# The copy of q's and k's transposes queued two half chunks behind them, and the transposes five half chunks behind the rotation

## The chip, the cores and the metric

The kernel runs on one core of one Trainium2 chip. The metric is the device time of one execution in microseconds, a median of three runs.

## The reference

One trunk layer on 256 rows of 2048 numbers, all in float32. The part in which the change lies is the projection and the attention:

```
xn = rms_norm(h, norm1_g[l])
proj = jnp.einsum('bsd,dn->bsn', xn, w_in[l].astype(xn.dtype))
q, k, v, ga, gg = jnp.split(proj, ...)
q = apply_rope(rms_norm(q, q_norm_g[l]), cos, sin)
k = apply_rope(rms_norm(k, k_norm_g[l]), cos, sin)
att = diff_attention(q, k, v, lam)
att = rms_norm(att, subln_g[l]) * (1.0 - lambda_init)
u = silu(layer_norm(causal_depthwise_conv(ga * sigmoid(gg))))
h = h + concat([att, u]) @ w_out
h = h + (silu(hn @ w_gate) * (hn @ w_up)) @ w_down      # hn = rms_norm(h, norm2_g)
```

There are 4 heads; each has two pairs of q and k of 128 columns, two softmaxes that are subtracted, and 256 columns of v.

## The kernel before

Every weight matrix is streamed in chunks of two 128-row slices by 512 columns. Each chunk is rounded by ScalarE (`whi`, line 320) and the remainder is taken by VectorE (`wlo`, line 329). TensorE then multiplies a chunk in two halves: eight matmuls with `whi` (lines 359 and 360) and four with `wlo` (line 365). The casts of chunk t+2 and its remainder are queued before chunk t is multiplied; `whi` and `wlo` have three buffers each.

All the other work is written as generators. `multiply` calls `resume()` after each half of a chunk, and each running generator then puts its next instructions into the engines' queues; `lag(n)` lets n half chunks pass. So the order on each engine is fixed when the program is built, and an instruction that must wait holds everything behind it on its engine. The taps of the depthwise convolution (`y`, line 517, on VectorE) are dealt out in `run_side` between the chunks.

w_in's columns come in the order convolution, k and q of heads 0 and 1, k and q of heads 2 and 3, then v. For each block of k or q, `qk_rows` runs twice, once for each 128 rows: square sums on ScalarE (line 427), `fq` from them on GpSimd (lines 217, 218, 615), the scaled `qn` on ScalarE (line 619), the rotation on VectorE (lines 626 to 629), four transposes on TensorE (`ps_qk`, line 634), and a copy of the bank to `qT` or `kT` on ScalarE (line 635). When all of a pair of heads are placed, `attend_scores` runs per head: scores `ps_s` (line 649, two banks), their maximum on VectorE (`nmx`, line 659), exponents on ScalarE (`pr`, line 668), `r` on VectorE (line 677), `a` on GpSimd (line 679), `p` on ScalarE (line 688), the weights `wt` on VectorE (line 695), transposes `ps_wt` (line 701) and their copy to `qT` (line 706). `attend_values` then multiplies with v (`ps_o`, line 727; v is copied out of its banks at line 712), scales the result (`att`, line 738), transposes it (`ps_at`, line 746) and splits it into `mahi` on ScalarE (line 233) and `malo` on VectorE (line 234).

All these small products share four banks of PSUM (`AUX = 4`, tag `aux`). `room(n, hold)` lets a generator wait at build time until n of the four can be had, and `held` counts those that stay taken over several half chunks.

Of the kernel before, what the change touches and what calls it, by code (L numbers as in the profile page):

```python
# [63 lines left out]
RAW_BUFS = 5  # L64
AUX = 4

LAG = (3, 2, 6)
HL_BUFS = 3

KTILE_US = 1.30  # L70
# [52 lines left out]
def tile_block(  # L123
# [89 lines left out]
    def rsqrt_mean(dst, ss, n, eps):  # L213

        k = dst.shape[-1]
        t = small.tile([P, 8], F32, tag="rsq", name="rsq")
        pool.tensor_scalar(t[:, :k], ss, 1.0 / n, eps, ALU.mult, ALU.add)
        pool.tensor_tensor(dst, t[:, :k], neghalf[:, :k], ALU.pow)
# [31 lines left out]
    def lag(n):  # L250
        for _ in range(n):
            yield


    held = [0]

    def room(n, hold=0):
        while held[0] + n > AUX:
            yield
        held[0] += hold  # L260
# [6 lines left out]
    def spend(us):  # L267
        credit[0] -= us
# [156 lines left out]
    def square_sum(src, accum, **kw):  # L425
        junk = pre.tile([P, N], F32, tag="junk", name="junk", bufs=1)
        act.activation(junk[:, : src.shape[-1]], src, AF.Square, accum_out=accum, **kw)
# [162 lines left out]
    def qk_done(key, b, ps):  # L590
        for m in range(NM):
            yield
            start(qk_rows(key, b, m, ps[m]))
            yield
        if key == "q":
            while not all((k, b, m) in placed for k in "qk" for m in range(NM)):
                yield
            if b == 0:
                negative_lambda()
            for hd in (2 * b, 2 * b + 1):  # L600
                start(attend_scores(hd))
                yield from lag(4)
# [3 lines left out]
    def qk_rows(key, b, m, ps):  # L606

        G = N // DH
        spend(1.65)
        ss = small.tile([P, G], F32, tag="ssq", name="ssq")  # L610
        for j in range(G):
            square_sum(ps[:, j * DH : (j + 1) * DH], ss[:, j : j + 1], scale=rstd1[m])
        f = small.tile([P, G], F32, tag="fq", name="fq")
        rsqrt_mean(f, ss, DH, EPS)
        pool.tensor_scalar(f, f, rstd1[m], 0.0, ALU.mult, ALU.add)
        yield from lag(LAG[0])
        qn = pre.tile([P, G, DH], F32, tag="va", name="qn")
        for j in range(G):
            act.activation(qn[:, j, :], ps[:, j * DH : (j + 1) * DH], AF.Copy, scale=f[:, j : j + 1])
        yield from lag(LAG[1])  # L620
        t1 = pre.tile([P, G, DH], F32, tag="vb", name="t1")
        t2 = pre.tile([P, G, DH], F32, tag="vc", name="t2")
        tab = gcs[key, m]
        hd = DH // 2
        bc = lambda ap, n: ap.unsqueeze(1).to_broadcast([P, G, n])
        dve.tensor_tensor(t1, qn, bc(tab[:, 0, :], DH), ALU.mult)
        dve.tensor_tensor(t2[:, :, :hd], qn[:, :, hd:], bc(tab[:, 1, :hd], hd), ALU.mult)
        dve.tensor_tensor(t2[:, :, hd:], qn[:, :, :hd], bc(tab[:, 1, hd:], hd), ALU.mult)
        dve.tensor_tensor(t1, t1, t2, ALU.add)
        yield from lag(LAG[2])  # L630
        yield from room(1)
        pt = aux_ps.tile([P, G, P], F32, tag="aux", name="ps_qk")
        for j in range(G):
            pe.transpose(pt[:, j, :], t1[:, j, :], ident)
        act.copy(qkT[key][:, b * G : (b + 1) * G, m * P : (m + 1) * P], pt)
        placed.add((key, b, m))

# [609 lines left out]
```

## Time and profile before

| | |
|---|---|
| median of 3 runs | 1048.91 us (1048.85 to 1048.91) |
| the profiled execution | 1048.92 us, of which the span is 1047.1 us |
| TensorE clock granted | 1.00 |
| q, k and attention in the span | about 120 to 270 us |
| DMA, mean over the span | 221 GB/s |

A matmul's row shows a start and a length; the lengths overlap, since the next one enters while the last one drains. What counts is the distance from start to start. In brackets behind a row of the timeline stands how long the engine had nothing to do before it, and whose instruction ended that.

### The profile page before, as it was taken

The page shows a single profiled execution, that of the slowest core. Times are in us where ns is not written, and L with a number is a line of the kernel's source. Part 1 is how long each engine was busy: PE and PEld are TensorE (multiplying, and loading weights), DVE is VectorE, ACT ScalarE, POOL GpSimd, SP SyncE. Part 2 cuts the span into 40 slices and gives each one's busy share as a digit, 9 for nine tenths or more (in the row PEclk, how much of TensorE's full clock was granted, in tenths as well). Part 3 has the DMA queues.
Part 4 walks back from the last instruction along what each step waited for, and adds up shares of the span by engine and source line. Part 5 has one row for each costly group of instructions (what it writes and reads, how often), then busy time and mean ns, then how long its engine had stood idle before and what let it go on. Part 6 is the DMA issues. An engine that isn't in the chain of part 4 may idle for free.

```text
span 1047.1 us, 12933 instructions
## 1 busy us (share of the span) xinstructions
PE 1036.2 (99%) x4663; PEld 852.5 (81%) x4663; DVE 900.6 (86%) x1095; ACT 621.6 (59%) x786; POOL 100.5 (10%) x143
## 2 busy tenths in 40 slices
PE   9999999999999999999999999999999999999998
PEld 7888887877788788888888888888888888888886
DVE  7899889898765599999787898999878789989897
ACT  7544666755756565776463657666644446657442
POOL 0130122201100100000001010000000110000010
PEclk9999999999999999999999999999999999999999
DMA  9657654453546566987867789879757879798683
GB/s 335 227 182 280 212 163 167 154 181 134 177 153 226 194 223 214 268 266 236 232 210 188 217 271 273 256 217 285 248 175 241 219 208 291 222 287 267 187 265 85
DMA packets 113936, 231.30 MB, mean 221 GB/s; under 512 B 7504, under 2 KB 8656, under 8 KB 113616
## 3 DMA queue, kind: packets, MB, share of 16 engines
q1 hardware_dynamic: 104864, 203.71, 56.9%
q0 software_dynamic: 8864, 26.74, 13.4%
q8 instruction: 36, 0.59, 0.2%
q14 instruction: 28, 0.23, 0.1%
q10 hardware_dynamic: 144, 0.03, 0.0%
HBM read 204.24 MB, written 9.44 MB: 204 GB/s over the span
## 4 chain that ended last, share of the span: by engine, by line
PE 61%; DMA 2%; DVE 2%; issue 1%; ACT 0%; DVEq 0%; POOLq 0%
PE q L1020 12%; PE q L1014 12%; PE q L1015 12%; PE q L995 8%; PE q L993 7%; PE q L994 7%; DMA raw<-in_w_down_dram 1%; PE ps_a L831 1%; DMA wlo<-raw 1%; PE acc L365 1%; PE acc L359 1%; PE acc L360 1%; DVE wlo L329 1%; DVE wlt L976 0%; DVE wt L966 0%
## 5 line engine op out<-in xcount | busy, mean ns | idle before, releaser
L320 ACT CAST whi<-raw 128x1024 fp32r<-128x1024 f32 (+1 forms) x273 | 281.5, 1048 | 141.6 <-PE acc L360 58.9
L329 DVE TENSOR_TENSOR wlo<-raw,whi 128x1024 fp32r<-128x1024 f32 (+1 forms) x239 | 287.8, 1218 | 73.5 <-ACT whi L320 73.3
L972 ACT CAST wh<-wt 128x2048 fp32r<-128x2048 f32 x52 | 99.6, 1914 | 77.6 <-DVE wt L968 76.9
L976 DVE TENSOR_TENSOR wlt<-wt,wh 128x2048 fp32r<-128x2048 f32 x52 | 119.1, 2290 | 14.9 <-ACT wh L972 14.7
L359 PE MATMUL acc<-whi,xhi 128*128 128x512 f32 x320 | 126.9, 397 | 1.0 <-ACT whi L320 0.9
L360 PE MATMUL acc<-whi,xlo 128*128 128x512 f32 x320 | 125.2, 391 | 0.0
L1014 PE MATMUL q<-whi,chi 128*128 128x512 f32 x320 | 125.2, 391 | 0.0
L1015 PE MATMUL q<-whi,clo 128*128 128x512 f32 x320 | 124.5, 389 | 0.0
L993 PE MATMUL q<-wh,fhi 128*128 128x512 f32 x280 | 109.9, 393 | 0.0
L994 PE MATMUL q<-wh,flo 128*128 128x512 f32 x280 | 109.1, 390 | 0.0
L517 DVE SCALAR_TENSOR_TENSOR y<-upad,cw,y 128x256 f32<-128x256 f32 x240 | 102.2, 482 | 2.2 <-ACT y L510 2.2
L1014 PE MATMUL q<-whi,ahi 128*128 128x512 f32 x256 | 100.2, 391 | 0.0
L1015 PE MATMUL q<-whi,alo 128*128 128x512 f32 x256 | 99.6, 389 | 0.0
L975 DVE TENSOR_TENSOR wlb<-wb,wh 128x1536 fp32r<-128x1536 f32 x52 | 91.1, 1752 | 1.8 <-ACT wh L969 1.8
L365 PE MATMUL acc<-wlo,xhi 128*128 128x512 f32 x320 | 87.8, 396 | 2.0 <-DVE wlo L329 2.0
L1020 PE MATMUL q<-wlo,chi 128*128 128x512 f32 x320 | 85.7, 390 | 0.2 <-DMA wlo<-raw 0.2
L969 ACT CAST wh<-wb 128x1536 fp32r<-128x1536 f32 x52 | 76.6, 1474 | 0.0
L365 PEld LDWEIGHTS acc<-wlo,xhi 128*128 128x128 f32 x320 | 59.7, 189 | 15.3 <-DVE wlo L329 3.3
L359 PEld LDWEIGHTS acc<-whi,xhi 128*128 128x128 f32 x320 | 60.4, 189 | 14.3 <-ACT whi L320 1.9
L1020 PEld LDWEIGHTS q<-wlo,chi 128*128 128x128 f32 x320 | 59.9, 188 | 13.2 <-DMA wlo<-raw 0.8
L360 PEld LDWEIGHTS acc<-whi,xlo 128*128 128x128 f32 x320 | 60.4, 189 | 12.2
L1014 PEld LDWEIGHTS q<-whi,chi 128*128 128x128 f32 x320 | 60.1, 188 | 12.3
(230 smaller groups left out, 1739.1 us busy)
## 6 DMA issues: line engine op xcount, KB each, us to landing
raw<-in_w_in_dram SPq DMA_DIRECT2D x79, 512.0 KB, 4.6
raw<-in_w_down_dram SPq DMA_DIRECT2D x64, 512.0 KB, 7.2
raw<-in_w_gate_dram SPq DMA_DIRECT2D x48, 512.0 KB, 7.5
raw<-in_w_up_dram SPq DMA_DIRECT2D x48, 512.0 KB, 6.2
wb<-in_w_up_dram SPq DMA_DIRECT2D x40, 512.0 KB, 3.7
wb<-in_w_gate_dram SPq DMA_DIRECT2D x40, 512.0 KB, 4.9
wlo<-raw POOLq DMA_DIRECT2D x34, 512.0 KB, 7.1
raw<-in_w_out_dram SPq DMA_DIRECT2D x32, 512.0 KB, 4.2
```

The costliest lines, as they stand in the source:

```text
L320: act.copy(c["hi"], c["raw"])
L329: dve.tensor_tensor(c["lo"], c["raw"], c["hi"].bitcast(F32), ALU.subtract)
L359: pe.matmul(ps[m], xhi[:, ms], hi[:, j, :], start=c["first"] and j == 0, stop=False)
L360: pe.matmul(ps[m], xlo[:, ms], hi[:, j, :], start=False, stop=False)
L365: pe.matmul(ps[m], xhi[:, ms], lo[:, j, :], start=False, stop=c["last"] and j == nk - 1)
L517: dve.scalar_tensor_tensor(y[:, ct, :], src, wk, y[:, ct, :], ALU.mult, ALU.add)
L976: dve.tensor_tensor(lot, c["t"], c["hi"][:, :SUMMED].bitcast(F32), ALU.subtract)
L993: pe.matmul(ps, hi, c["hi"][:, w], start=bool(first), stop=False)
L994: pe.matmul(ps, lo, c["hi"][:, w], start=False, stop=False)
L1014: pe.matmul(ps, xs[i][0][:, ms], hi[:, i, :], start=i == 0 and bool(c["first"].get(qs[m])), stop=False)
L1015: pe.matmul(ps, xs[i][1][:, ms], hi[:, i, :], start=False, stop=False)
L1020: pe.matmul(sum_bank(c, qs[m]), xs[i][0][:, ms], lo[:, i, :], start=False, stop=i == 1 and bool(c["last"].get(qs[m])))
```

## The change

The transposes of a rotated block are put into the queue five half chunks behind the rotation and no longer six. The copy out of their bank, which stood directly behind them, comes two half chunks later, and the bank counts as held in between. Seen from the rotation the copy stands at seven half chunks and no longer at six.

```
-LAG = (3, 2, 6)
+LAG = (3, 2, 5)
+COPY_LAG = 2
...
         yield from lag(LAG[2])
-        yield from room(1)
+        yield from room(1, 1)
         pt = aux_ps.tile([P, G, P], F32, tag="aux", name="ps_qk")
         for j in range(G):
             pe.transpose(pt[:, j, :], t1[:, j, :], ident)
+        yield from lag(COPY_LAG)
+        held[0] -= 1
         act.copy(qkT[key][:, b * G : (b + 1) * G, m * P : (m + 1) * P], pt)
         placed.add((key, b, m))
```

The lines after the change carry other numbers: 1 more from line 68 on, and 3 more behind the transposes. Three places show what moves.

TensorE, at the second transposes of q of heads 0 and 1 (`t_1546` is the rotated block). Before, they stand behind the chunk's four matmuls with `wlo`:

```order
L359 MATMUL acc<-whi,xhi_313 128x512
L360 MATMUL acc<-whi,xlo_314 128x512
L365 MATMUL acc<-wlo,xhi_313 128x512 x4
L634 MATMUL ps_qk<-ident,t_1546 128x128 x4
L359 MATMUL acc<-whi,xhi_140 128x512
```

With the change they stand between the two halves:

```order
L360 MATMUL acc<-whi,xhi_313 128x512
L361 MATMUL acc<-whi,xlo_314 128x512
L635 MATMUL ps_qk<-ident,t_1546 128x128 x4
L366 MATMUL acc<-wlo,xhi_313 128x512 x4
L360 MATMUL acc<-whi,xhi_140 128x512
```

The transposes have moved ahead of the four matmuls that use `wlo`. It is the same for the second transposes of q of heads 2 and 3.

ScalarE, where heads 0 and 1 are multiplied with v and the scores of head 2 wait for their exponents. `junk,sso` are square sums of `ps_o`. Before:

```order
L427 ACTIVATE junk,sso<-ps_o 128x256 x4
L320 CAST whi<-raw 128x1024
L738 ACTIVATE att<-ps_o,ro 128x256 x2
L668 ACTIVATE pr,sm<-ps_s,nmx 128x128 x2
L668 ACTIVATE pr,sm<-ps_s,nmx 128x256 x2
L233 ACTIVATE mahi<-ps_at,cols 128x256 x2
L738 ACTIVATE att<-ps_o,ro 128x256 x2
L320 CAST whi<-raw 128x1024
L233 ACTIVATE mahi<-ps_at,cols 128x256 x2
```

With the change:

```order
L428 ACTIVATE junk,sso<-ps_o 128x256 x4
L321 CAST whi<-raw 128x1024
L741 ACTIVATE att<-ps_o,ro 128x256 x2
L234 ACTIVATE mahi<-ps_at,cols 128x256 x2
L741 ACTIVATE att<-ps_o,ro 128x256 x2
L321 CAST whi<-raw 128x1024
L671 ACTIVATE pr,sm<-ps_s,nmx 128x128 x2
L671 ACTIVATE pr,sm<-ps_s,nmx 128x256 x2
L234 ACTIVATE mahi<-ps_at,cols 128x256 x2
```

The exponents `pr` of head 2, which empty the two banks of its scores, have moved behind `mahi`, the second `att` and a cast. On TensorE the scores of head 3 stand directly behind the first `ps_at` in both programs.

ScalarE, at the copy of head 2's transposed weights `ps_wt`, on which `ps_o` of head 2 waits. Before:

```order
L688 ACTIVATE p_2491<-pr,a_2462 128x128
L688 ACTIVATE p_2493<-pr,a_2466 128x256
L706 COPY qT<-ps_wt 128x384
L712 ACTIVATE v_133<-acc,rstd_0_122 128x512
L712 ACTIVATE v_134<-acc,rstd_1_123 128x512
L320 CAST whi<-raw 128x1024 x2
L427 ACTIVATE junk,sso<-ps_o 128x256 x2
```

With the change:

```order
L691 ACTIVATE p_2491<-pr,a_2463 128x128
L691 ACTIVATE p_2493<-pr,a_2467 128x256
L715 ACTIVATE v_133<-acc,rstd_0_122 128x512
L715 ACTIVATE v_134<-acc,rstd_1_123 128x512
L321 CAST whi<-raw 128x1024
L709 COPY qT<-ps_wt 128x384
L321 CAST whi<-raw 128x1024
L428 ACTIVATE junk,sso<-ps_o 128x256 x2
```

The copy has moved behind the two copies of v and a cast. `p` here belongs to head 3.

On VectorE the work is the same; some taps and the small operations of the softmax change places. Between the maximum of head 3's scores and its `r` there are ten taps with the change and nine before, and in the stretch of two remainders `wlo` that ends with the `wlo` of the chunk at which q of heads 2 and 3 is transposed for the second time there are five with the change and six before. The orders of GpSimd and SyncE are unchanged, and behind the attention those of all engines are.

## The prediction

> **What bounds the kernel now.** I read the page first: which engine is busy, and who stands in the chain that ended last. Then the waits summed by pair (microseconds in total, times, the longest), to see where TensorE still waits in the part that the change moves, and what ScalarE waits for.
>
> ```profile
> PE 1036.2 (99%) x4663; PEld 852.5 (81%) x4663; DVE 900.6 (86%) x1095; ACT 621.6 (59%) x786; POOL 100.5 (10%) x143
> ...
> PE 61%; DMA 2%; DVE 2%; issue 1%; ACT 0%; DVEq 0%; POOLq 0%
> ...
> PE acc L365 <- DVE wlo L329: 2.0, 2, 1.2
> PE ps_o L727 <- ACT qT L706: 0.6, 1, 0.6
> PE ps_o L727 <- ACT v L712: 0.3, 1, 0.3
> ...
> ACT qT L635 <- PE ps_qk L634: 12.0, 4, 3.2
> ACT kT L635 <- PE ps_qk L634: 6.5, 3, 3.0
> ```
>
> TensorE is 99% busy and the change gives it no matmul more or less. The time can move only by TensorE's waits, and nearly all waits of the stretch stand here: 2.0 us for `wlo` in two places, 0.9 us for `ps_o` in two. The 18.5 us that ScalarE waits in the copies are large, but ScalarE is busy 59% of the span. They count only where a late ScalarE delays VectorE's `wlo` or a bank. The bank held for two half chunks costs nothing by itself: it is a count kept while the program is built, and shows only as the order of what follows, the scores and all behind them half a chunk later. SyncE's and GpSimd's queues keep their order, so loads move only with what they wait for. So my sum is made of four places on TensorE, in order of time.
>
> **The change part by part: the two waits for `wlo`.** These are TensorE's rows at the second transposes of q, first for heads 0 and 1, then for heads 2 and 3.
>
> ```profile
> 164.74 1.20 PE L365 MATMUL acc<-wlo,xhi 128*128 128x512 f32 x4 [0.80 <-DVE wlo L329]
> 165.78 0.60 PE L634 MATMUL ps_qk<-ident,t 128*128 128x128 f32 x4
> 166.13 0.48 PE L359 MATMUL acc<-whi,xhi 128*128 128x512 f32 x1
> ...
> 215.39 1.20 PE L365 MATMUL acc<-wlo,xhi 128*128 128x512 f32 x4 [1.24 <-DVE wlo L329]
> ```
>
> TensorE waits 0.80 and 1.24 in front of the four matmuls with `wlo`; the transposes behind them take 0.35 (165.78 to 166.13). With the change the transposes stand ahead of those matmuls, so each 0.35 falls into a wait. That is sure where the rotated block is ready in time. At the second place VectorE also has one tap less in front of this `wlo`. What else can shorten the waits is VectorE coming there earlier:
>
> ```profile
> 138.52 0.59 ACT L635 COPY kT<-ps_qk 128x512 f32<-128x512 f32 x1 [3.01 <-PE ps_qk L634]
> ...
> 152.31 1.14 ACT L619 ACTIVATE qn<-acc,fq 128x128 f32<-128x128 f32 x4 [1.61 <-POOL fq L615]
> ...
> 154.42 1.23 DVE L329 TENSOR_TENSOR wlo<-raw,whi 128x1024 fp32r<-128x1024 f32 x1 [3.39 <-ACT whi L320]
> 161.89 1.67 DVE L517 SCALAR_TENSOR_TENSOR y<-upad,cw,y 128x256 f32<-128x256 f32 x4
> 163.47 1.22 DVE L329 TENSOR_TENSOR wlo<-raw,whi 128x1024 fp32r<-128x1024 f32 x1
> ```
>
> Four taps start 1.58 apart from the next `wlo` (161.89 to 163.47), so a tap is 0.40. ScalarE stood 3.01 in front of the copy at 138.52, with the square sums and casts behind it in its queue; the copy two half chunks later has its transposes long done. The square sums, `fq`, `qn` and the cast that VectorE waits 3.39 for can all come earlier, but at 152.31 it is GpSimd's `fq` that ends the wait, so not by 3.01. Bounds for both places together: at least 0.40 + 0.35 = 0.75 (TensorE comes to the second place earlier by what the first gave, so that 0.35 isn't counted twice), at most 0.80 + 1.24 = 2.04. I see no row that says where between, and take the middle, **-1.40**.
>
> **The scores of head 3.** They stand directly behind the first `ps_at` in both programs. Head 2's scores hold two of the four banks until ScalarE's `pr` has read them. Rows of TensorE, ScalarE and VectorE there:
>
> ```profile
> 231.77 0.60 PE L746 MATMUL ps_at<-ident,att 128*128 128x128 f32 x4
> 232.21 1.60 PE L649 MATMUL ps_s<-kT,qT 128*128 128x128 f32 x8
> ...
> 232.03 0.50 ACT L668 ACTIVATE pr<-ps_s,nmx 128x256 f32<-128x256 f32 x1
> 232.48 0.51 ACT L233 ACTIVATE mahi<-ps_at,cols 128x256 fp32r<-128x256 f32 x1
> 233.54 0.47 ACT L233 ACTIVATE mahi<-ps_at,cols 128x256 fp32r<-128x256 f32 x1 [0.55 <-DVE malo L234]
> ...
> 233.02 0.48 DVE L234 SCALAR_TENSOR_TENSOR malo<-ps_at,cols,mahi 128x256 fp32r<-128x256 f32 x1 [0.21 <-ACT mahi L233]
> 234.04 0.48 DVE L234 SCALAR_TENSOR_TENSOR malo<-ps_at,cols,mahi 128x256 fp32r<-128x256 f32 x1 [0.54 <-ACT mahi L233]
> ```
>
> Before, the last `pr` (232.03) frees the second bank just as TensorE needs it, and the scores follow `ps_at` by 0.44. With the change `pr` stands behind `mahi`, `att` and a cast, so the banks of head 2 are still full. Head 3 can take only the bank of head 1's `ps_o` (free with the second `att`) and that of this `ps_at`, free when the second `malo` has read it. The four small steps mahi, malo, mahi, malo follow one another at half a microsecond each, and end at 234.04 + 0.48 = 234.52, which is 2.75 behind `ps_at`. So a new wait of 2.75 - 0.44 = 2.31 stands in front of the scores. I take **+2.2**, since the scores themselves stretch a little over the wait now (1.60) and would not then. Bounds: a tap of 0.40 less or more around the second `malo`, 1.8 to 2.6. TensorE's matmuls for the chunk, VectorE's `wlo` and ScalarE's casts queue behind this wait. Behind it TensorE stands at -1.40 + 2.2 = +0.8.
>
> **`ps_o` of head 2.** It needs head 2's `qT` copy, which the change puts behind both copies of v and a cast.
>
> ```profile
> 249.38 0.90 ACT L688 ACTIVATE p<-pr,a 128x128 f32<-128x128 f32 x2 [3.99 <-POOL a L679]
> 250.19 0.46 ACT L706 COPY qT<-ps_wt 128x384 f32<-128x384 f32 x1
> 250.55 1.27 ACT L712 ACTIVATE v<-acc,rstd 128x512 f32<-128x512 f32 x2
> 251.70 2.01 ACT L320 CAST whi<-raw 128x1024 fp32r<-128x1024 f32 x2
> ...
> 251.29 1.56 PE L727 MATMUL ps_o<-v,qT 128*128 128x256 f32 x6 [0.28 <-ACT v L712]
> ```
>
> Before, `ps_o` starts 1.91 behind head 3's `p` (249.38 to 251.29), having waited 0.28 for v. With the change the order is `p` 0.81, v 1.15, one cast 1.00 (half of 2.01), copy 0.46, together 3.42: **1.51 more**. To that comes how far `p` itself moves. ScalarE waits 3.99 for it, and what it waits for goes back over GpSimd's `a` to VectorE's `r`. VectorE's rows, and those it is tied to:
>
> ```profile
> 235.49 0.60 PE L746 MATMUL ps_at<-ident,att 128*128 128x128 f32 x4
> ...
> 236.12 0.48 ACT L233 ACTIVATE mahi<-ps_at,cols 128x256 fp32r<-128x256 f32 x1 [0.44 <-PE ps_at L746]
> ...
> 236.03 1.22 DVE L329 TENSOR_TENSOR wlo<-raw,whi 128x1024 fp32r<-128x1024 f32 x1
> 237.16 0.48 DVE L234 SCALAR_TENSOR_TENSOR malo<-ps_at,cols,mahi 128x256 fp32r<-128x256 f32 x1
> 238.19 0.48 DVE L234 SCALAR_TENSOR_TENSOR malo<-ps_at,cols,mahi 128x256 fp32r<-128x256 f32 x1 [0.54 <-ACT mahi L233]
> ...
> 248.69 0.22 DVE L677 RECIPROCAL r<-sm 128x2 f32<-128x2 f32 x2
> ```
>
> From 238.59 to 248.69 VectorE has no gap. The anchor is the second `malo` of head 1, which follows the second `ps_at`, at +0.8. Before, its first `malo` stood at 237.16 behind a `wlo`, though `mahi` was done at 236.60; with VectorE earlier than TensorE now, that `wlo` is out of the way and 0.55 is saved. One tap more in front of `r` costs 0.40. So `p` moves by 0.8 - 0.55 + 0.40 = +0.65, and `ps_o` by 1.51 + 0.65 = **+2.16**. TensorE itself would come at 0.8 - 0.28 = +0.52, so its wait there is 1.64. Behind this the orders are the same and all of it carries to the end: TensorE has no slack to give it back.
>
> The sum goes against the profiled execution's own 1048.92 (span 1047.1, 1.8 outside it), 0.01 from the median: 1048.92 + 2.16 = **1051.1**. Ends: with 2.04 gained and 1.8 lost TensorE is at -0.24, `p` at -0.39, the end at +1.1, or 1050.0; with 0.75 gained and 2.6 lost +1.85, `p` +1.70, +3.2, or 1052.1.
>
> **The rivals.** *The copy is hidden.* Head 2's `qT` copy comes late, but `p` comes so much earlier that TensorE has not arrived: VectorE would have to reach `r` 1.64 earlier than by the rows above. For it: `r` depends on my anchor alone. Against: VectorE has no gap in the ten microseconds in front. TensorE is then at +0.52: 1049.4, not measurably slower than before.
>
> *The banks come free in time.* If head 3's scores find two free banks, the wait at 232 doesn't come. It turns on whether `pr` of head 2, or the second `malo`, ends by the time of `ps_s`. TensorE is then at -1.40, `p` at about -1.55, `ps_o` at -0.04: 1048.9; and 1048.92 - 1.40 - 0.28 = 1047.2 to 1046.6 if the copy is hidden as well. Against it stand the four banks and the order of ScalarE. This, with the copy hidden, is the only way to a faster kernel that I see.
>
> *GpSimd is held out again.* `fq` for q goes through GpSimd:
>
> ```profile
> 148.50 3.40 POOL L218 TENSOR_TENSOR fq<-rsq,neghalf 128x4 f32<-128x4 f32 x1
> 152.63 1.01 POOL L218 TENSOR_TENSOR fq<-rsq,neghalf 128x4 f32<-128x4 f32 x1
> ...
> 148.68 2.35 DVE L329 TENSOR_TENSOR wlo<-raw,whi 128x1024 fp32r<-128x1024 f32 x2
> ```
>
> The same operation takes 1.01 alone and 3.40 while VectorE runs two `wlo` without a break: 2.4 more. With square sums earlier, `fq` meets other operations of VectorE. If it is held as long as before or longer, the gain of 1.40 doesn't come. TensorE is then at +2.2, `p` at +2.05, the end at +3.56: 1052.5; if such 2.4 reach TensorE once more, 1054.9. [...]
>
> **How the numbers follow.** My forecast has 0.64, the hidden copy 0.15, the free banks 0.07, GpSimd 0.14. About 0.2%, or 2.1 us, is what a measurement of this kernel can tell from no change: slower means above 1051.0, faster below 1046.8. The forecast's range of 1050.0 to 1052.1 has a little over half above 1051.0 (0.36), and GpSimd's case all (0.14): slower 0.50. The rest of the forecast (0.28), the hidden copy and most of the free banks (0.04) make 0.47 within; 0.03 is left for faster. The range goes from 1048.9, where the banks alone are free, to 1053.0, half a microsecond above GpSimd's lower time; it leaves out both rivals' far ends, about 0.1.
>
> **What would show it.** In the changed trace: the waits for `wlo` near 164 and 215 together 0.75 or more shorter, with the transposes ahead of them; a wait of about 2 us in front of `ps_s` near 231, ended by `malo` or `att`; a wait of about 1.6 in front of `ps_o` near 252, ended by the `qT` copy; from there a constant lag of about 2 us. No wait at `ps_s`, or a lag that grows behind 260, would prove the prediction wrong; so would a wait for `wlo` that has moved to another chunk.

## The result and the profile after

The changed kernel takes 1056.5 us (median of 6 runs, 1055.55 to 1057.58) against 1048.91: slower by 7.6 us, ratio 1.0071, 95% interval 1.006 to 1.0082. The direction was forecast, the size (+2.2) not: the time lies 3.5 us above the range. The profiled execution is one of 1056.62 with a span of 1054.8.

The page of the changed kernel, the engines' busy time and then TensorE's waits (us in total, times, the longest):

```profile
PE 1038.4 (98%) x4663; PEld 854.5 (81%) x4663; DVE 900.8 (85%) x1095; ACT 621.7 (59%) x786; POOL 101.6 (10%) x143
...
PE ps_o L730 <- ACT qT L709: 4.2, 2, 3.6
PE ps_s L652 <- DVE malo L235: 2.5, 1, 2.5
...
PE acc L366 <- DVE wlo L330: 1.0, 1, 1.0
```

The 2.0 us of waits for `wlo` are now 1.0, and two waits are new or larger: 2.5 in front of `ps_s`, and up to 3.6 in front of `ps_o`. TensorE's busy time has grown by 2.2 us with the same 4663 instructions: some of them ran slower. TensorE's timeline shows the four places:

```profile
164.48 1.17 PE L366 MATMUL acc<-wlo,xhi 128*128 128x512 f32 x4
...
214.63 1.19 PE L366 MATMUL acc<-wlo,xhi 128*128 128x512 f32 x4 [0.95 <-DVE wlo L330]
...
230.54 0.60 PE L749 MATMUL ps_at<-ident,att 128*128 128x128 f32 x4
233.61 1.55 PE L652 MATMUL ps_s<-kT,qT 128*128 128x128 f32 x8 [2.47 <-DVE malo L235]
...
236.84 0.60 PE L749 MATMUL ps_at<-ident,att 128*128 128x128 f32 x4
...
249.78 0.50 PE L360 MATMUL acc<-whi,mahi 128*128 128x512 f32 x1 [0.54 <-ACT whi L321]
...
256.81 2.93 PE L730 MATMUL ps_o<-v,qT 128*128 128x256 f32 x6 [3.63 <-ACT qT L709]
...
263.71 0.39 PE L360 MATMUL acc<-whi,mahi 128*128 128x512 f32 x1
...
294.46 0.50 PE L360 MATMUL acc<-whi,mchi 128*128 128x512 f32 x1 [0.57 <-DVE mchi L583]
```

Read each start against the same instruction before. At the first `ps_at` TensorE is 1.23 early (230.54 against 231.77): that is the gain of the earlier transposes. At `ps_s` it is 1.40 late, at `ps_o` 5.52 late (256.81 against 251.29). Then `ps_o` itself takes 2.93 where it took 1.56. The stretches of half a microsecond say why; the number behind POOL's is the granted TensorE clock:

```profile
255.00:255.50 0.50, 0.00 (x0) 0.00 (x0) 0.28 (x1) 0.50 (x2) 0.00 (x0) 1.00 0.71 246
255.50:256.00 0.50, 0.00 (x0) 0.00 (x0) 0.00 (x0) 0.50 (x1) 0.00 (x0) 0.74 1.02 291
256.00:256.50 0.50, 0.00 (x0) 0.00 (x0) 0.10 (x1) 0.50 (x2) 0.00 (x0) 0.50 0.91 233
...
262.00:262.50 0.50, 0.50 (x2) 0.33 (x1) 0.00 (x0) 0.00 (x0) 0.00 (x0) 0.50 0.00 0
262.50:263.00 0.50, 0.50 (x3) 0.41 (x2) 0.00 (x0) 0.02 (x1) 0.00 (x0) 0.94 0.00 0
```

In the middle of the wait the granted clock falls to half and stays there for 6.8 us (255.74 to 262.56, from the shares 0.74 and 0.94). TensorE works through most of that. Behind it the lag is 8.26, 2.74 more, read at TensorE's first matmul with `mchi` (294.46). Before:

```profile
286.20 0.50 PE L359 MATMUL acc<-whi,mchi 128*128 128x512 f32 x1 [0.58 <-DVE mchi L582]
```

By the end 0.56 of it has come back, which I did not follow up: 7.70.

Why `ps_o` is 5.52 late is told by GpSimd's, ScalarE's and VectorE's rows, in this order:

```profile
244.70 1.95 POOL L682 TENSOR_TENSOR a<-r,neg_lam 128x1 f32<-128x1 f32 x2 [15.53 <-DVE r L680]
251.80 1.94 POOL L682 TENSOR_TENSOR a<-r,neg_lam 128x1 f32<-128x1 f32 x2 [5.16 <-DVE r L680]
...
246.68 0.51 ACT L691 ACTIVATE p<-pr,a 128x256 f32<-128x256 f32 x1 [1.12 <-POOL a L682]
...
248.68 2.00 ACT L321 CAST whi<-raw 128x1024 fp32r<-128x1024 f32 x2
252.25 0.40 ACT L691 ACTIVATE p<-pr,a 128x128 f32<-128x128 f32 x1 [1.57 <-POOL a L682]
253.78 0.51 ACT L691 ACTIVATE p<-pr,a 128x256 f32<-128x256 f32 x1 [1.13 <-POOL a L682]
254.19 1.25 ACT L715 ACTIVATE v<-acc,rstd 128x512 f32<-128x512 f32 x2
255.33 1.04 ACT L321 CAST whi<-raw 128x1024 fp32r<-128x1024 f32 x1
256.27 0.48 ACT L709 COPY qT<-ps_wt 128x384 f32<-128x384 f32 x1
...
244.46 0.22 DVE L680 RECIPROCAL r<-sm 128x2 f32<-128x2 f32 x2
244.60 0.86 DVE L518 SCALAR_TENSOR_TENSOR y<-upad,cw,y 128x256 f32<-128x256 f32 x2
245.38 1.22 DVE L330 TENSOR_TENSOR wlo<-raw,whi 128x1024 fp32r<-128x1024 f32 x1
...
249.76 1.23 DVE L330 TENSOR_TENSOR wlo<-raw,whi 128x1024 fp32r<-128x1024 f32 x1 [1.58 <-ACT whi L321]
```

GpSimd's rows for `a` before, of heads 1, 2 and 3:

```profile
193.27 1.95 POOL L679 TENSOR_TENSOR a<-r,neg_lam 128x1 f32<-128x1 f32 x2 [6.87 <-DVE r L677]
...
239.61 0.34 POOL L679 TENSOR_TENSOR a<-r,neg_lam 128x1 f32<-128x1 f32 x2 [9.22 <-DVE r L677]
248.93 0.81 POOL L679 TENSOR_TENSOR a<-r,neg_lam 128x1 f32<-128x1 f32 x2 [8.98 <-DVE r L677]
```

The pair of products `a` of heads 2 and 3 takes 1.95 and 1.94; before it took 0.34 and 0.81. VectorE now puts two taps and a `wlo` directly behind `r`, and the second `a` ends only when that `wlo` does (246.65 and 246.60). ScalarE waits for it with the second `p` at 246.68; behind that stand `pr` of head 3 and the casts of 248.68, and for the first of these VectorE waits 1.58 at 249.76, so that head 3's `r` is late. Then the same happens to `a` and `p` of head 3, and behind that `p` come v, a cast and the copy on which `ps_o` waits.

### The profile page after: what moved, and what is told of

Same layout as the page of the kernel before. It is cut to its first block, busy times and chain, and to the rows that moved or that the text cites. A ratio compares the mean times of both kernels' runs of the same rounds, so it can differ in the third digit from the quotient of the medians.

```text
span 1054.8 us, 12936 instructions
## 1 busy us (share of the span) xinstructions
PE 1038.4 (98%) x4663; PEld 854.5 (81%) x4663; DVE 900.8 (85%) x1095; ACT 621.7 (59%) x786; POOL 101.6 (10%) x143
## 4 chain that ended last, share of the span: by engine, by line
PE 63%; DVE 1%; issue 0%; ACT 0%; DVEq 0%
PE q L1017 12%; PE q L1018 12%; PE q L1023 12%; PE q L998 8%; PE q L996 8%; PE q L997 8%; PE acc L366 1%; PE ps_a L834 1%; PE acc L360 1%; PE acc L361 1%; DVE wlo L330 0%; DVE wlt L979 0%; DVE wt L969 0%; ACT wh L975 0%; DVE wt L970 0%
## 5 line engine op out<-in xcount | busy, mean ns | idle before, releaser
L1018 PEld LDWEIGHTS q<-whi,clo 128*128 128x128 f32 x320 | 60.1, 188 | 12.3
```

The costliest lines, as they stand in the source:

```text
L1018: pe.matmul(ps, xs[i][1][:, ms], hi[:, i, :], start=False, stop=False)
```

## The experiments

They ran on three chips, four on each, on which the kernel before takes 1048.2 to 1048.3 us (median); what counts is the difference to it on the same chip. A time is a median too, and the rows are those of one profiled execution.

**Transposes at five, copy at six.** ScalarE's order is that of the kernel before; only the transposes stay early.

```diff
-COPY_LAG = 2
+COPY_LAG = 1
```

> The changed kernel with the copy queued one half chunk behind the transposes and not two: transposes at five half chunks behind the rotation, copy at six, where it stood before. ScalarE's order is then that of the kernel before. If the loss comes from the copy (and with it the scores and all behind them) coming half a chunk later, only the gain of the earlier transposes is left (TensorE was 1.23 us earlier at the first ps_at of the changed kernel): no wait in front of ps_s near 232, clock 1.00, about 1047.7 us (1047.2 to 1048.5). If the earlier transposes themselves do the harm, the time stays above 1051.

Measured 1047.01 against 1048.32, ratio 0.9988 (0.9979 to 0.9998). Two of TensorE's rows:

```profile
214.25 1.20 PE L366 MATMUL acc<-wlo,xhi 128*128 128x512 f32 x4 [0.74 <-DVE wlo L330]
...
249.85 1.56 PE L730 MATMUL ps_o<-v,qT 128*128 128x256 f32 x6 [0.40 <-ACT v L715]
```

No wait for `ps_s`, and 0.40 in front of `ps_o`. The loss belongs to the later copy and what it shifts; the earlier transposes are a gain.

**Filling the wait.** In the changed kernel, ahead of `ps_o`'s own matmuls and into its bank:

```diff
+        if hd == 2:
+            for _ in range(16):
+                pe.matmul(o[:, 0, :P], ident, ident, start=True, stop=True)
```

> The changed kernel with 16 extra matmuls of 128x128 (about 0.11 us each by the distance of the ps_wt rows, so 1.8 us) put into the wait of 3.63 us in front of ps_o of head 2; their result is overwritten. Theory (one long wait of TensorE makes the granted clock fall): the wait splits into 1.8 of work and about 1.9 of waiting, the granted clock stays at 1.00, ps_o starts at the same 256.8, and the 2.7 us lost behind it are back: about 1053.8 us (1053.3 to 1054.3). Rival (the clock falls from all the waits between 230 and 257 together, or for another reason): clock 0.89 over 240 to 270 as now and 1056 us or more.

Measured 1054.15 (1052.9 to 1055.09, 4 runs) against 1048.32, so +5.8 and not +7.6. TensorE and two stretches:

```profile
252.06 3.73 PE L730 MATMUL ps_o<-ident 128*128 128x128 f32 x32
255.88 1.56 PE L733 MATMUL ps_o<-v,qT 128*128 128x256 f32 x6
...
260.02 0.39 PE L360 MATMUL acc<-whi,mahi 128*128 128x512 f32 x1
...
256.00:258.00 2.00, 2.00 (x10) 1.72 (x11) 2.00 (x5) 1.26 (x4) 0.00 (x0) 1.00 0.74 256
258.00:260.00 2.00, 2.00 (x10) 1.66 (x9) 2.00 (x5) 1.14 (x3) 1.37 (x2) 1.00 0.69 254
```

I had mis-sized the filling: a product of these is two passes, and 32 passes fill the whole 3.7 us. `ps_o` starts no later (23.20 behind `ps_s`, as without the filling), the clock stays at 1.00, and from `ps_o` to the next chunk it is 4.14 (255.88 to 260.02) against 6.90 (256.81 to 263.71). That is 2.76 for the clock, which makes the theory's size. The profiled execution is the fastest of the four, 1052.9; the two slowest have a mean granted clock of 0.998, this one 1.000, so the spread over 2.2 us is probably that of the ninth run below: a fall of the clock in some executions and not in others.

**`a` on VectorE.** In the changed kernel, and, as a control, in the kernel before:

```diff
-            pool.tensor_tensor(a1, r[:, 1:2], neg_lam, ALU.mult)
+            dve.tensor_tensor(a1, r[:, 1:2], neg_lam, ALU.mult)
```

> The changed kernel with the small product a (128x1, twice per head) on VectorE directly behind r and not on GpSimd. Theory (GpSimd's a took 1.95 at 244.70 and 1.94 at 251.80, held out while VectorE ran taps and wlo, against 0.34 and 0.81 before; this delays p, the cast behind it and so VectorE's wlo): the wait of 1.58 of VectorE at 249.76 goes or shrinks to under 0.5, p comes 2 to 3 us earlier, the wait in front of ps_o shrinks from 3.63 to 0.8 to 1.6, the granted clock stays at 1.00, and the time is 1051.0 to 1052.3 us. Rival (the wait in front of ps_o is the copy standing behind v and a cast, and a is beside the path): the wait stays above 3 and the time at 1055.5 or more.

> The kernel before with a on VectorE as in the run above, as its control. Before, a took 0.34 and 0.81 for heads 2 and 3. p of head 3 comes up to 0.7 earlier, but ps_o of head 2 waited only 0.28 for v. Theory: the 0.28 goes at most, and two more small operations on VectorE cost nothing on TensorE: 1048.4 to 1049.0 us. Rival (VectorE is so full that two small operations per pair of rows move its wlo): slower by 0.3 or more.

Measured 1051.35 and 1048.95 against 1048.32: ratios 1.0026 (1.0017 to 1.0035) and 1.0008 (0.9999 to 1.0017). TensorE in the changed kernel with it:

```profile
232.57 1.55 PE L652 MATMUL ps_s<-kT,qT 128*128 128x128 f32 x8 [2.42 <-DVE malo L235]
...
253.03 1.56 PE L730 MATMUL ps_o<-v,qT 128*128 128x256 f32 x6 [1.75 <-ACT qT L709]
```

The wait in front of `ps_o` shrinks from 3.63 to 1.75, a little more than I had expected to remain, and in this execution, one of 1050.26, the clock behind it stays at 1.00. VectorE's 1.58 is gone. So GpSimd's late `a` is what made the forecast's 1.64 into 3.63. The time is less clean than the rows: the four fastest of the ten executions (1049.22 to 1050.45) have a mean clock of 0.999 or 1.000, the other six (1051.0 to 1052.99) 0.996 to 0.998. So the median lies in my range only because the clock falls in more than half of them; where it doesn't, the loss is 0.9 to 2.1 us. The control gains nothing; its small loss can't be told from none.

**`pr` of head 2 earlier.** In the changed kernel:

```diff
-        yield from lag(3)
+        yield from lag(2 if hd == 2 else 3)
```

> The changed kernel with head 2's exponents pr one half chunk earlier (two half chunks behind the maximum and not three), so that ScalarE reads the two banks ahead of mahi, as before; what follows for head 2 is half a chunk earlier too, and ScalarE's order from there on is that of the kernel before. Theory (banks not freed, then the late copy): the wait of 2.47 us in front of ps_s goes, the copy of head 2's weights stands ahead of v again, the wait in front of ps_o is under 1 us, the clock stays at 1.00, and the gain of the earlier transposes is left: about 1047.7 us (1047.0 to 1048.5). Rival (the scores of head 3 wait for another bank, or ps_o for something else): 1050 or more.

Measured 1046.98 against 1048.33, ratio 0.9986 (0.9977 to 0.9996). `ps_s` doesn't wait, and

```profile
249.78 1.56 PE L730 MATMUL ps_o<-v,qT 128*128 128x256 f32 x6 [0.42 <-ACT v L715]
```

The later copy by itself does no harm. It does harm through head 2's exponents and what follows them, which it queues half a chunk later, and one number for that head takes all of it back.

**v's copies later.** In the changed kernel v's second half is copied half a chunk later, so that the copy of the weights stands ahead of it.

```diff
         yield
+        if b == 1:
+            yield
```

> The changed kernel with the copies of v's second half one half chunk later, so that head 2's weights are copied ahead of v. It leaves the wait at ps_s and GpSimd's a as they are. Theory by the rows: the copy comes behind a cast but ahead of v, so v is the last that ps_o waits for: cast 1.0, copy 0.46, v 1.2 are the same work in another order, and ps_o does not start much earlier; the wait stays at 3 to 3.7 and the time between 1053.5 and 1056.6, the lower end if the wait falls short of what lowers the clock. Rival (what counts is the copy being behind v): the wait shrinks by 1.5 to about 2.1, the clock stays at 1.00, and 1052.3 us.

Measured 1054.57 against 1048.33, +6.2. The wait is 3.06 and the clock falls in it (0.94 over 240 to 270). It ends with v as expected, but stands in front of the next chunk's first matmul, which writes the bank that v is copied out of; `ps_o` now comes behind that half chunk, at 259.18, without a wait:

```profile
255.83 0.79 PE L360 MATMUL acc<-whi,mahi 128*128 128x512 f32 x1 [3.06 <-ACT v L717]
```

The rival, that the place of the copy behind v is the matter, is out: with the copy ahead of v TensorE still waits, for the chain in front of both.

**Each part alone.** First the transposes at five with the copy directly behind them, then the transposes at six with the copy at eight.

```diff
-COPY_LAG = 2
+COPY_LAG = 0
...
-        yield from room(1, 1)
+        yield from room(1)
...
-        held[0] -= 1
```

> The first part of the change alone: transposes five half chunks behind the rotation, the copy directly behind them again and no bank held. All the attention is then half a chunk earlier than before. Theory: ScalarE waits in the copies as before (3 us each), so VectorE gains less in front of wlo; the scores and the copy of the weights come no later: between 1047 and 1050 us. If the earlier transposes are what costs, 1051 or more.

```diff
-LAG = (3, 2, 5)
+LAG = (3, 2, 6)
```

> The second part of the change alone: transposes at six half chunks as before, the copy two half chunks behind them, at eight. The scores come half a chunk later still than in the changed kernel. Theory (later scores cost): a wait in front of ps_s or of ps_o remains, 1050 to 1057 us. Rival (only the combination at seven half chunks meets the crossing of pr with mahi): 1049 or less.

Measured 1050.51 (ratio 1.0016, 1.0007 to 1.0026) and 1057.32 (1.0088, 1.0071 to 1.0105) against 1048.33. TensorE's largest wait of the first, and two of the second:

```profile
286.58 0.49 PE L360 MATMUL acc<-whi,mchi 128*128 128x512 f32 x1 [1.69 <-DVE mchi L583]
```

```profile
236.02 0.67 PE L749 MATMUL ps_at<-ident,att 128*128 128x128 f32 x4 [0.84 <-DVE malo L235]
...
240.16 2.04 PE L652 MATMUL ps_s<-kT,qT 128*128 128x256 f32 x4 [3.03 <-DVE malo L235]
```

For the first I was wrong twice. No wait for `wlo` is left at 164 or 215, so ScalarE's waiting in the copies did not limit the gain; and `mchi`, behind the attention, now makes TensorE wait 1.69, before 0.58. The clock falls to half behind that wait (288.22 to 291.64). Four of the ten executions have a mean clock of 0.999 or 1.000 and take 1048.44 to 1049.61, six have 0.997 or 0.998 and take 1050.51 to 1051.82, so most of the loss goes with the clock. Why `mchi` is later I did not try. It isn't the earlier attention as such, since the second kernel, with the attention later, has the same wait of 1.69 there (294.11) and keeps its clock: the matmuls from 294.90 to 296.06 take 0.39 to 0.40, where those at half take 0.63. In both, VectorE's statistics of the convolution (line 549) stand behind one more `wlo` than before; that this is the cause is not shown. Otherwise the second is the changed kernel's trouble at `ps_s`, larger: the wait is 3.03, and the clock is 0.72 over 240 to 250. In front of head 2's `ps_o` it waits only 0.57.

**`pr` late and nothing else.** The kernel of the first experiment, with head 2's `pr` moved behind `mahi`, `att` and a cast, as in the changed kernel, and `r` kept in its place:

```diff
-        yield from lag(3)
+        yield from lag(4 if hd == 2 else 3)
...
-        yield from lag(2)
+        yield from lag(1 if hd == 2 else 2)
```

> The kernel of the first run above (transposes at five half chunks, copy at six; 1047.01 us there) with one thing moved: head 2's exponents pr stand behind mahi, the second att and a cast on ScalarE, as in the changed kernel, and r follows at its old place. The orders of TensorE, VectorE and GpSimd are the same. Theory (head 2's scores keep two of the four banks until pr): a wait of 2.3 to 2.6 us in front of ps_s of head 3, ended by malo, and nothing else: a stays short, the copy of head 2's weights stays ahead of v, clock 1.00, 1048.5 to 1049.7 us. Rival (the wait at ps_s comes from something else in the change): no wait there and 1047.0.

Measured 1048.97 against 1046.57 for the kernel it comes from on the same chip: +2.4. TensorE and three stretches of the profiled execution, one of 1050.32:

```profile
233.05 2.90 PE L652 MATMUL ps_s<-kT,qT 128*128 128x128 f32 x8 [2.42 <-DVE malo L235]
...
232.00:234.00 2.00, 0.95 (x4) 0.98 (x5) 1.58 (x4) 2.00 (x5) 0.00 (x0) 0.68 0.80 256
234.00:236.00 2.00, 2.00 (x7) 1.64 (x6) 1.62 (x3) 1.67 (x9) 0.00 (x0) 0.50 0.02 7
236.00:238.00 2.00, 2.00 (x11) 1.59 (x11) 0.00 (x0) 0.00 (x0) 0.00 (x0) 0.97 0.00 0
```

The wait is there with nothing else moved: the four banks and `pr`'s place make it. A surprise stands in the stretches: after a wait of 2.42 the clock is at half for 3.4 us, though the changed kernel's 2.47 in the same place left it at 1.00. By the mean granted clock of each execution, six of this kernel's ten have 0.999 or 1.000 and take 1048.09 to 1049.12, four have 0.998 and take 1049.11 to 1050.32. The six without the fall are 2.0 slower than the kernel they come from.

**A shorter filling.** As the second experiment, with 4 products instead of 16.

```diff
-            for _ in range(16):
+            for _ in range(4):
```

> The changed kernel with four extra products (eight passes of 128x128 at 0.12 us by the rows of the run with 16, about 0.9 us) in front of ps_o of head 2; the wait behind them is left at about 2.7 us. It tells how long a wait has to be: the clock fell at 3.63, 3.06 and 3.03 and stood at 2.47. If a wait must be near 3 us, the granted clock stays at 1.00 and the time is as with 16 products. If 2.7 is enough, the clock falls to 0.50 for some us behind it and the time is as in the changed kernel.

Measured 1055.26 (1053.54 to 1056.56, 4 runs) against 1048.19. The profiled execution is the fastest of the four, its clock 1.00 behind the wait:

```profile
256.47 1.56 PE L733 MATMUL ps_o<-v,qT 128*128 128x256 f32 x6 [2.75 <-ACT qT L709]
```

The two slowest have a mean clock of 0.996, this one 0.999. Only this one is traced, so which wait the others lost their clock at is not shown. But the question was put wrongly: by the ninth run and this one no single length decides. The clock can fall at a wait of 2.42 and stay up at one of 2.75; the last section has what the traces show of it.

**Transposes at four, and the best once more.** Both with the copy at six; the second is the first experiment's kernel.

```diff
-LAG = (3, 2, 5)
+LAG = (3, 2, 4)
```

> Transposes four half chunks behind the rotation, the copy two behind them, so at six as before. Against the kernel with five and six only TensorE's order differs: the transposes stand a half chunk earlier still, behind the wlo matmuls and not ahead of them. Theory (a third of a microsecond of transposes inside a wait for wlo is what the early transposes gain, besides ScalarE's earlier copies): the waits at 164 and 214 come back in part, 1047.2 to 1048.5 us, not faster than with five and six. Rival (earlier is better as long as the copy stays): below 1046.8.

> The kernel with transposes at five half chunks and the copy at six once more, for a closer interval and on the same chip as the run with four. As in the first run: a ratio of 0.9988 to the kernel before, between 0.998 and 0.9995.

Measured 1046.43 and 1046.57 against 1048.19: ratios 0.9983 (0.9974 to 0.9992) and 0.9986 (0.9977 to 0.9995). Both beat both kernels; between them no difference can be told. With four, TensorE's wait has only changed its name, so my expectation of a loss was wrong:

```profile
211.50 0.63 PE L635 MATMUL ps_qk<-ident,t 128*128 128x128 f32 x4 [0.69 <-DVE t L630]
```

## Why the prediction was wrong

**The two waits for `wlo`** (-1.40): right. TensorE was 1.23 early at `ps_at`, one wait gone and the other 0.95, and the kernels that keep the early transposes with ScalarE's old order around the attention gain 1.3 to 1.6 us.

**The scores of head 3** (+2.2, bounds 1.8 to 2.6): right in cause and nearly in size. The distance from `ps_at` grew from 0.44 to 3.07, by 2.63; in the ninth run it costs 2.4 by itself, 2.0 where the clock doesn't fall.

**The order in front of `ps_o`**: right. From v to `ps_o` I had added 1.15, 1.00 and 0.46, which is 2.61; it took 2.62 (254.19 to 256.81).

**How far `p` moves** (+0.65): this step failed. Measured +2.87 (249.38 to 252.25), and then 1.13 more between the two halves of `p`. It rested on the sentence that VectorE has no gap from head 1's `malo` to head 3's `r`. The `malo` came 0.82 later where I had 0.25, because TensorE stood at +1.35 at the second `ps_at` (236.84 against 235.49) and not at +0.8. The tap cost its 0.40, but the rest is a new gap of 1.58. I took the gapless VectorE of the kernel before for a property of the work. It was one of the order: before, head 2's `r` was followed by the maximum of head 3's scores, and GpSimd's `a` took 0.34; with `r` behind them, two taps and a `wlo` follow, and it took 1.95. I moved `r` past nothing on GpSimd because GpSimd's own order had not changed. What VectorE runs beside it had. The trace before had a sign of it that I didn't read: head 1's `a` took 1.95 at 193.27, with a tap and a `wlo` behind its `r`. The rival that named GpSimd had a lengthening of this kind (3.40 against 1.01), at 0.14, and put it at `fq`, where it did not matter: the `fq` of 3.40 took 1.29 in the changed kernel (148.04).

**The wait of 1.64** was therefore 3.63, although TensorE itself came to it at +1.89 where I had +0.52: 0.60 of that is from `ps_s`, and 0.54 is a new wait for a cast that stands behind the late `p` of head 2 (249.78). And **the clock** was a term that the sum did not have: 2.74 in the profiled execution, 2.76 by the filling. Terms and result: -1.23 + 2.63 makes +1.40 at `ps_s`; the chain over `a`, `p`, v and the copy makes +5.52 at `ps_o`; the clock makes +8.26; 0.56 comes back.

What stays open: why 0.56 comes back behind the attention, and what moves `mchi` in the two kernels that take one part of the change alone.

## What to carry to other kernels

When a small operation changes its place, look not only at what stands in front of it and behind it in its own queue, but at what now runs on VectorE while GpSimd does the next step; a pair of products of 128x1 took 1.95 us there and 0.34 before. Price a new wait of TensorE with the slower clock that may follow it, as a chance and not as a certainty: here the clock fell at five waits of 1.69 to 3.63 us and stayed at 1.00 at others of 1.69 to 2.75. And a delay between two dependent steps can be chosen per step: here an earlier producer with the consumer left in its place won 1.3 to 1.6 us, where the consumer moved back by half a chunk lost 7.6.

## What the runs showed of the hardware

GpSimd's pair of products `a` (128x1) took 0.34 beside VectorE's memsets and reductions on `ps_s` (239.61 before), 0.81 beside three taps (248.93 before), and 1.94 to 1.95 where two taps and, without a gap, a `wlo` came behind `r` (244.70 and 251.80 in the changed kernel); the second product then ended with the `wlo`. With the copy at eight that `wlo` starts only at 247.75, and the pair, beside two taps from 246.94, took 0.81. With one tap and a `wlo` behind `r` it took 1.95 too and ended with the next tap (193.27 before).

The granted clock fell to half in or behind waits of 3.63, 3.06, 3.03, 2.42 and 1.69 us, and stayed at 1.00 at others of 2.75 (the shorter filling), 2.47 (the changed kernel) and, with the copy at eight, 1.69. The five falls, from the shares of the stretches of half a microsecond and TensorE's waits (us):

| | fall | TensorE idle in the 3.41 us ahead of it | waiting still behind it | time at half |
|---|---|---|---|---|
| changed kernel | 255.74 | 2.56 | 1.07 | 6.82 |
| v's copies later | 255.47 | 2.70 | 0.36 | 3.42 |
| copy directly behind the transposes | 288.22 | 1.69 | 0 | 3.42 |
| copy at eight | 238.74 | 2.30 | 1.42 | 6.83 |
| `pr` late | 232.72 | 2.08 | 0.33 | 3.41 |

In the kernel with the copy directly behind the transposes the clock fell only when TensorE had been working again for 1.64 us (the wait ends at 286.58):

```profile
287.50:288.00 0.50, 0.50 (x4) 0.41 (x3) 0.50 (x2) 0.09 (x1) 0.00 (x0) 1.00 1.04 344
288.00:288.50 0.50, 0.50 (x3) 0.36 (x3) 0.50 (x1) 0.00 (x0) 0.00 (x0) 0.72 0.79 303
```

The clock's records in the traces have stretches of 1041.065 us at full clock in the kernel before, and of 249.173 at full, 6.827 at half and 791.892 at full in the changed one: 305, 73, 2 and 232 times 3.4133. The stretch of 791.892 ends at 1054.46, behind the last matmul, where the clock falls again. My estimate from this, with steps of 3.4133 counted back from 255.74: the changed kernel's wait of 2.47 is cut at 231.85, 0.71 in one step and 1.76 in the next, and the clock stayed; the copy at eight's wait of 1.69, counted on from the end of its slow time at 245.57, is cut at 293.36 into 0.94 and 0.75, and the clock stayed there too. Idle time within one step doesn't decide alone: 1.69 went with a fall and 1.76 with none. What makes the steps, and how much idle time a fall takes, is not shown.
